# Two numbers per pass: fewer pairs of units block by block at the heads and tails of the input projections

## The chip, the cores and the metric

The kernel runs on one core of one Trainium2 chip. The metric is the device time of one execution in microseconds (us). The engines are named as the profile names them: PE is TensorE (PEld its weight loads), DVE is VectorE, ACT is ScalarE, POOL is GpSimd, SP is SyncE, which here only issues transfers.

## The reference

A trunk of two layers is applied with the same weights to two requests: a prompt of 512 tokens and a sample of 2048 tokens, each of width 1024.

```python
def trunk(x, ...):
    for l in range(DEPTH):                       # DEPTH = 2
        y = even_layer(x, w_in_even, ...) if l % 2 == 0 else odd_layer(x, w_in_odd, ...)
        x = layer_norm(ALPHA * x + y, ln_g[l], ln_b[l])

def even_layer(x, w_in, sink, w_out, t5_table):
    qa, ka, va, qb, kb, vb, ga, gb = _split(x @ w_in, EVEN_SPLITS)
    ...
    return concatenate([oa * silu(ga), ob * silu(gb)]) @ w_out

def odd_layer(x, w_in, rpb, lb, gnorm, w_out):
    qc, kc, vc, qd, idd, zf, zb, gc, gd = _split(x @ w_in, ODD_SPLITS)
    ...
    return concatenate([oc * silu(gc), od * silu(gd)]) @ w_out
```

What is left out is mixer A (windowed attention) and mixer B (dilated attention) in the even layer, mixer C (neighbourhood attention) and mixer D (HGRN2, both directions) in the odd one. This case concerns the first line of each layer, the combined input projection `x @ w_in`, in float32.

## The kernel before

**Tokens and units.** The 2560 tokens are 5 blocks of 512: block 0 is the prompt, blocks 1 to 4 are the sample. The columns of `w_in` are cut into units of 128, named after the reference's splits (`qb`, `kb`, ...; `v0`, `v1`, `v2` are value columns), and two units are a pair. Layer 0 has 14 pairs, layer 1 has 16.

**One pair.** A pair on a block is computed by seven matrix products of half size in place of eight (a fast scheme). x and the weights are each split into a high and a low float32r part, and each product takes three matmuls for each of four quarters of the contraction: 84 matmuls of 128 x 256 for a pair on one block, twice as many for a pair on two blocks (`pair_fm`, line 305; value pairs in `pair_v`, line 405). VectorE and ScalarE add the products out of PSUM (`products`, lines 270 to 281; the last additions are at lines 318 to 352): these are the evictions, and they cover one block (256 columns) or two (512).

**Weights.** `weights` (from line 160) is a generator that prepares the seven weight operands (`whl`) of a pair, in the order of the list `work`, into a pool of 6 tiles. The first time a pair comes, the raw weights are loaded, VectorE forms the sums, ScalarE and GpSimd split them (lines 106 and 107), and four of the seven prepared tiles, 512 KB each, are also written to DRAM. When the pair comes again, the four are read back (line 204), and of the raw weights 512 KB and 256 KB (lines 176 and 177); the other three operands are split anew. One preparation serves both blocks of a pair that runs on two.

**x.** `load_x` fills `xh` and `xl` of one block, seven forms of four quarters `k`, through a ring of two raw tiles. There are two such buffers, for even and odd blocks.

```python
        for k in range(4):
            r = raw(k)
            yield
            self.split(xh[:, k, :3], xl[:, k, :3], r[:, 1:])
            yield
            sums(k, r)
            yield
            self.split(xh[:, k, 3:], xl[:, k, 3:], r)
            yield
```

The raw load of 512 KB is issued at line 131 on SP; `split` is one instruction on ScalarE (line 106) and one on VectorE (line 107, tile `xl`, 128 x 768 and then 128 x 1024); `sums` are four subtractions on VectorE (lines 135 to 138). The generator advances two steps after each product (`tick`). The first two products of a pair (X11 and X21) need only the 128 x 768 parts.

**The order of the pairs.** `group` writes the part of the list for two blocks:

```python
        start[len(work)] = g[1]
        work += [(p, [b]) for b in g for p in pairs[:head]]
        work += [(p, list(g)) for p in pairs[head:len(pairs) - tail]]
        work += [(p, [g[0]]) for p in pairs[len(pairs) - tail:]]
        start[len(work)] = then
        work += [(p, [g[1]]) for p in pairs[len(pairs) - tail:]]
```

The first `head` pairs run on the first block alone, during which the second block's x is loaded, and then on the second block; the middle pairs run on both; the last `tail` pairs run on the first block, and then on the second, during which the next pass's first x (block `then`) is loaded into the buffer that came free. A pair in a head or tail is a *step* of 84 matmuls, and its weights are prepared twice. Each layer has a pass over blocks 0 and 1, one over 2 and 3, and then block 4 alone, whose steps a scheduler mixes with mixer A (layer 0) or mixer D (layer 1). The instructions' order on each engine is set by the scheduler from the program's order; transfers all stand in SP's queue in that order.

Of the kernel before, what the change touches and what calls it, by code (L numbers as in the profile page):

```python
# [67 lines left out]
def drain(g):  # L68
    for _ in g:
        pass  # L70


class Trunk:
# [1244 lines left out]
    def layer0(self):  # L1318
        pj, p0, p1, px, ma, bk, bw = (ExitStack() for _ in range(7))
        self.rp = self.pool(pj, "rp0", 2, side="left")  # L1320
        self.proj_pools(pj, 0, "left")
        x = [self.pool(e, f"x{i}", 1, side="left") for i, e in enumerate((p0, p1))]
        self.more_ps(p1, 0, "left")
        ring = self.pool(px, "xr0", 2, side="left")
        pair = {n: self.pairs(0, (n,)) for n in ("qa", "ka", "ga", "kb", "v0", "v2", "qb", "gb")}
        pairs = pair["v2"] + pair["kb"][2:3] + pair["kb"][0:1] + pair["kb"][1:2] + pair["ga"] + pair["gb"] + pair["v0"] + pair["qa"] + pair["ka"] + pair["qb"]
        work, start = [], {}
        self.group(work, start, (0, 1), pairs, 4, 3, 2)
        self.group(work, start, (2, 3), pairs, 4, 3, 4)
        work += [(p, [4]) for p in self.pairs(0, ("kb", "ga", "v0", "qa", "ka", "gb", "v2", "qb"))]  # L1330
        xs = {}
        load = lambda b: self.load_x(0, b, x[b % 2], [ring], xs)
        with ExitStack() as e:
            x0 = self.load_x(0, 0, x[0], [ring, self.pool(e, "xs", 2, side="right")], xs)
            self.proj_begin(0, work, {i: (lambda b=b: load(b)) for i, b in start.items()})
            next(x0)
            self.wq += [next(self.wgen), next(self.wgen)]
            drain(x0)
        self.side = self.side_work()
        n = len(work) - len(pairs)  # L1340
        self.proj(0, n, xs)
        while 4 not in xs:
            self.tick()
        px.close()
        p1.close()
        self.pss.pop()
        self.lbt = self.lower_bounds(self.const)
        self.gn = self.const.tile([P, 4], F32, name="gn")
        self.nc.sync.dma_start(self.gn, self.A["gn"])
        drain(self.side)  # L1350
        self.proj(0, len(pairs), xs)
        p0.close()
        pj.close()
        self.mixer_a(ma)
        ma.close()
        self.b_open(bk)
        self.b_work(bw)
        with ExitStack() as s:
            b = self.mixer_b(((1, 2), (1, 1), (0, 2), (0, 1), (0, 0), (1, 0)))
            for _ in range(24):  # L1360
                next(b)
            self.out_open(s, 0, "right", range(6))
            drain(b)
            bw.close()
            self.out_work(s, 0, "right")
            out = self.output(0)
            cb, ob = ExitStack(), ExitStack()
            self.ob = self.pool(ob, "o_b", 2, side="right")
            comb = self.b_combine(cb)
            next(comb)  # L1370
            for i in range(1, NB):
                next(comb)
                for _ in range(4):
                    next(out)
            drain(comb)
            cb.close()
            bk.close()
            self.p1 = ExitStack()
            self.x = [self.pool(self.p1, "y0", 1, side="left")]
            self.rp = self.pool(self.p1, "rp1", 2, side="left")  # L1380
            self.xr = self.pool(self.p1, "xr1", 2, side="left")
            self.plan1()
            x0 = self.load_x(1, 0, self.x[0], [self.xr], self.xs)
            for _ in range(4):
                next(out)
                for _ in range(4):
                    next(x0, None)
            drain(x0)
            ob.close()
            self.wp = self.pool(self.p1, "wp1", 6, side="left")  # L1390
            self.wq.insert(0, self.next_w())
            drain(out)

    def plan1(self):
        self.cd, self.cc = self.pairs(1, ("zb", "v1", "zf", "qd", "gd")), self.pairs(1, ("kc", "v0", "qc", "gc"))
        work, start, self.xs = [], {}, {}
        order = self.pairs(1, ("kc", "gc", "zb", "zf", "gd", "v0", "v1", "qc", "qd"))
        self.group(work, start, (0, 1), order, 3, 4, 2)
        self.group(work, start, (2, 3), order, 3, 4, 4)
        work += [(p, [4]) for p in self.cd + self.cc]  # L1400
        load = lambda b: self.load_x(1, b, self.x[b % 2], [self.xr], self.xs)
        self.proj_begin(1, work, {i: (lambda b=b: load(b)) for i, b in start.items()})
# [129 lines left out]
```

## Time and profile before

| | |
|---|---|
| median of 3 runs | 3397.63 us (3362.09 to 3405.03) |
| the profiled execution | 3397.89 us |
| its span | 3396.1 us |
| TensorE busy | 3158.8 us, 93% |
| VectorE busy | 2135.2 us, 63% |
| ScalarE busy | 1350.9 us, 40% |
| GpSimd busy | 1292.4 us, 38% |
| DMA | 765.35 MB, 225 GB/s in the mean |
| mean granted clock of TensorE | 0.958 |

The busy time of an engine is the sum of its instructions; matmuls are pipelined, so a busy TensorE is not always one at its best rate. What the table can't tell is where TensorE stands still; for that the stretches around the borders of the passes are looked at apart. The clock is given as a share of the full 2.4 GHz; the lower level is 1.2 GHz, 0.5.

### The profile page before, as it was taken

To read this page: it belongs to the slowest core of one execution; us is meant where nothing else is said; L and a number is where in the kernel's file an instruction comes from. 1 tells how busy PE (TensorE), PEld (TensorE's weight loads), DVE (VectorE), ACT (ScalarE), POOL (GpSimd) and SP (SyncE) were. 2 spreads that over 40 slices of the span, in tenths; PEclk is the share of its full clock that TensorE was granted. 3 is DMA by queue.
4 is the path that set the end of the run, shared out by engine and by line. 5 is a ranking of instruction groups with operands and counts; after the bars stand their busy time and mean duration, and the time that the engine had idled before them with its cause. 6 is when DMAs were issued, how large, how long until landed. Compare 5 with 4: busy or idle time off the path is not lost.

```text
span 3396.1 us, 71726 instructions
## 1 busy us (share of the span) xinstructions
PE 3158.8 (93%) x26922; PEld 2711.5 (80%) x26922; DVE 2135.2 (63%) x5201; ACT 1350.9 (40%) x3182; POOL 1292.4 (38%) x1041
## 2 busy tenths in 40 slices
PE   6999689979999999999799999999889888989998
PEld 5999689977776566677699999999879866666787
DVE  8555533257666454599965475332797788885576
ACT  4323321235455565412333233211333367777510
POOL 6446341322221010055554463212464544343244
PEclk9999899989999787999899999999999989999999
DMA  6857995799988377546575599557979885545443
GB/s 244 292 209 263 316 344 198 261 285 260 264 233 221 92 184 165 143 153 216 195 295 207 209 327 350 200 192 258 339 259 315 299 237 141 147 135 174 136 145 113
DMA packets 518048, 765.35 MB, mean 225 GB/s; under 512 B 72923, under 2 KB 331611, under 8 KB 517447
## 3 DMA queue, kind: packets, MB, share of 16 engines
q1 hardware_dynamic: 494023, 739.79, 68.2%
q10 hardware_dynamic: 23680, 20.97, 1.8%
q8 instruction: 215, 3.52, 0.4%
q14 instruction: 130, 1.06, 0.1%
HBM read 529.09 MB, written 231.54 MB: 224 GB/s over the span
## 4 chain that ended last, share of the span: by engine, by line
PE 44%; DVE 13%; DMA 5%; issue 3%; ACT 2%; POOL 1%; SPq 0%; DVEq 0%; POOLq 0%; ACTq 0%
PE acc L305 16%; PE oacc L969 7%; PE acc L405 6%; PE bpv L705 3%; PE bpt L689 2%; DMA whl<-wk_f 2%; PE bs L661 2%; DVE dQ L1248 2%; PE cs L1083 1%; PE bs L660 1%; PE cpv L1115 1%; DMA dF<-fm_zf 1%; DVE dT L1237 1%; PE bs L671 1%; PE cpt L1100 1%
## 5 line engine op out<-in xcount | busy, mean ns | idle before, releaser
L305 PE MATMUL acc<-xh,whl 128*128 128x256 f32 x7560 | 1431.5, 288 | 109.9 <-DMA whl<-wk_f 53.6
L305 PEld LDWEIGHTS acc<-xh,whl 128*128 128x128 f32 x7560 | 1211.1, 195 | 135.6 <-issue 75.6
L305 PE MATMUL acc<-xl,whl 128*128 128x256 f32 x3780 | 1081.4, 286 | 8.5 <-DVE xl L107 8.5
L107 POOL TENSOR_TENSOR whl<-wraw,whl 128x512 fp32r<-128x512 f32 x447 | 611.5, 1380 | 809.7 <-ACT whl L106 769.3
L305 PEld LDWEIGHTS acc<-xl,whl 128*128 128x128 f32 x3780 | 736.9, 195 | 10.2 <-DVE xl L107 10.1
L106 ACT ACTIVATE whl<-wraw 128x512 fp32r<-128x512 f32 x447 | 277.9, 628 | 435.3 <-PE acc L305 163.4
L969 PE MATMUL oacc<-wohl,yh 128*128 128x512 f32 x960 | 312.0, 406 | 5.6 <-ACT yh L106 3.4
L405 PE MATMUL acc<-whl,xh 128*128 128x256 f32 x1680 | 307.5, 285 | 2.9 <-POOL whl L107 2.8
L270 DVE TENSOR_TENSOR u<-acc,u 128x256 f32<-128x256 f32 (+1 forms) x279 | 147.0, 527 | 227.6 <-PE acc L305 142.7
L405 PEld LDWEIGHTS acc<-whl,xh 128*128 128x128 f32 x1680 | 262.8, 192 | 6.0 <-POOL whl L107 3.2
L1247 POOL TENSOR_TENSOR dK<-dK,dT 128x512 f32<-128x512 f32 x120 | 158.8, 1332 | 223.0 <-ACT dKm L1215 91.2
L405 PE MATMUL acc<-whl,xl 128*128 128x256 f32 x840 | 238.3, 284 | 0.0
L969 PEld LDWEIGHTS oacc<-wohl,yh 128*128 128x128 f32 x960 | 180.5, 190 | 52.3 <-ACT yh L106 4.7
L969 PE MATMUL oacc<-wohl,yl 128*128 128x512 f32 x480 | 189.2, 399 | 1.3 <-DVE yl L107 1.3
L983 POOL TENSOR_TENSOR res<-res,gb 128x1024 f32<-128x1024 f32 (+2 forms) x40 | 94.2, 2354 | 225.0 <-DVE res L976 145.2
L405 PEld LDWEIGHTS acc<-whl,xl 128*128 128x128 f32 x840 | 161.6, 192 | 0.1
L278 ACT ACTIVATE u<-acc 128x256 f32<-128x256 f32 (+1 forms) x124 | 55.9, 451 | 224.2 <-PE acc L305 192.8
L326 ACT ACTIVATE sg<-evc 128x512 f32<-128x512 f32 (+1 forms) x128 | 70.5, 551 | 184.2 <-DVE evc L318 158.3
L318 DVE TENSOR_TENSOR evc<-acc,u 128x512 f32<-128x512 f32 (+1 forms) x140 | 79.7, 571 | 89.0 <-PE acc L305 84.2
L681 ACT ACTIVATE bss<-bss,bstat 128x128 f32<-128x128 f32 (+2 forms) x240 | 107.2, 449 | 70.6 <-DVE bstat L679 70.3
L106 ACT ACTIVATE xh<-xraw 128x768 fp32r<-128x768 f32 (+1 forms) x80 | 73.7, 946 | 145.3 <-DVE xraw L138 89.2
L679 DVE CUSTOM_DVE_ANT_0 bss<-bs,btab 128x256 f32<-128x256 f32 (+2 forms) x224 | 72.0, 359 | 89.1 <-PE bs L661 53.8
(1026 smaller groups left out, 5646.6 us busy)
## 6 DMA issues: line engine op xcount, KB each, us to landing
whl<-wk_f SPq DMA_DIRECT2D x328, 512.0 KB
wk_f<-whl SPq DMA_DIRECT2D x108, 512.0 KB
wraw<-w SPq DMA_DIRECT2D x82, 512.0 KB
wraw<-w SPq DMA_DIRECT2D x26, 1024.0 KB
whl<-wk_v SPq DMA_DIRECT2D x48, 512.0 KB
wraw<-w SPq DMA_DIRECT2D x86, 256.0 KB
vtri<-vc_d SPq DMA_DIRECT2D x60, 240.0 KB
bq<-fm_qb SPq DMA_DIRECT2D x50, 256.0 KB
```

The source lines that it names most:

```text
L106: nc.scalar.activation(h, src, AF.Copy)
L107: (eng_l or nc.vector).tensor_sub(l, src, h.bitcast(F32))
L270: nc.vector.tensor_add(d, a, u)
L305: nc.tensor.matmul(accs[0][:, i * 256:(i + 1) * 256], w[:, wi, k * P:(k + 1) * P], xv[:, k, x], start=(k == 0 and j == 0), stop=(k == 3 an ...
L318: nc.vector.tensor_add(c, a, u)
L405: nc.tensor.matmul(acc[:, t * 256:(t + 1) * 256], xv[:, k, x, t * P:(t + 1) * P], w[k // 2][:, wi, k % 2 * 256:(k % 2 + 1) * 256], start=( ...
L679: nc.vector.tensor_tensor_reduce(ss[h][:, i, :nk], sc[h][:, i, so[i]:so[i] + nk], tb[:, hh, :], 1.0, BIG, ALU.add, ALU.min, mcol)
L681: nc.scalar.activation(ss[h][:, i, :nk], ss[h][:, i, :nk], AF.Exp, scale=-1.0, bias=mcol, accum_out=stt[:, t, hh, 1:2])
L705: nc.tensor.matmul(pvt[64 * h:64 * h + 64, t - t4], v[:cn, h * 64:h * 64 + 64], pts[h][:cn, i, ci], start=(ci == 0), stop=(ci == len(chunk ...
L969: nc.tensor.matmul(acc, yv, wo[c][:, wi, cs], start=(c == chunks[0][0] and i == 0), stop=(c == chunks[-1][0] and i == 2))
L983: e.tensor_mul(r[:, c0:c1], r[:, c0:c1], gb[:, 0, c0:c1])
L1247: nc.gpsimd.tensor_mul(km, km, of(T_, nb + 1, -(nb + 1), 2, 0))
```

## The change

Only the numbers `head` and `tail` are changed: in the first call of `group` the tail alone, in the other three both.

```diff
--- before.py
+++ after.py
@@ -1325,8 +1325,8 @@
         pair = {n: self.pairs(0, (n,)) for n in ("qa", "ka", "ga", "kb", "v0", "v2", "qb", "gb")}
         pairs = pair["v2"] + pair["kb"][2:3] + pair["kb"][0:1] + pair["kb"][1:2] + pair["ga"] + pair["gb"] + pair["v0"] + pair["qa"] + pair["ka"] + pair["qb"]
         work, start = [], {}
-        self.group(work, start, (0, 1), pairs, 4, 3, 2)
-        self.group(work, start, (2, 3), pairs, 4, 3, 4)
+        self.group(work, start, (0, 1), pairs, 4, 2, 2)
+        self.group(work, start, (2, 3), pairs, 2, 2, 4)
         work += [(p, [4]) for p in self.pairs(0, ("kb", "ga", "v0", "qa", "ka", "gb", "v2", "qb"))]
         xs = {}
         load = lambda b: self.load_x(0, b, x[b % 2], [ring], xs)
@@ -1395,8 +1395,8 @@
         self.cd, self.cc = self.pairs(1, ("zb", "v1", "zf", "qd", "gd")), self.pairs(1, ("kc", "v0", "qc", "gc"))
         work, start, self.xs = [], {}, {}
         order = self.pairs(1, ("kc", "gc", "zb", "zf", "gd", "v0", "v1", "qc", "qd"))
-        self.group(work, start, (0, 1), order, 3, 4, 2)
-        self.group(work, start, (2, 3), order, 3, 4, 4)
+        self.group(work, start, (0, 1), order, 2, 2, 2)
+        self.group(work, start, (2, 3), order, 2, 2, 4)
         work += [(p, [4]) for p in self.cd + self.cc]
         load = lambda b: self.load_x(1, b, self.x[b % 2], [self.xr], self.xs)
         self.proj_begin(1, work, {i: (lambda b=b: load(b)) for i, b in start.items()})
```

In layer 0 the pass over blocks 0 and 1 has one step pair fewer in its tail, and the pass over 2 and 3 two fewer in its head and one fewer in its tail. In layer 1 each pass has one fewer in its head and two fewer in its tail. So 4 pairs of layer 0 and 6 of layer 1 now run over both blocks, with one preparation of weights in place of two. The number of matmuls stays the same. All transfers of weights that are left out are counted on SP: 40 of line 204 (512 KB), 10 of line 176 (512 KB) and 10 of line 177 (256 KB).

SP, layer 0, from the pass over blocks 0, 1 to that over 2, 3. `whl<-wk_f_0_n_m` are the reads of prepared weights (m grows by one within a pair: 3477 is the last pair of the tail, 142 the first of the next head), `xraw<-xT` the raw loads of block 2's x, whose first two quarters were issued in the pair ahead. Before:

```order
L204 DMA whl<-wk_f_0_2_3309 128x1024
L204 DMA whl<-wk_f_0_3_3310 128x1024
L376 DMA fm_qb<-evh 128x512 x2
L376 DMA fm_qb<-evo 128x512 x2
L176 DMA wraw<-w 128x1024
L177 DMA wraw<-w 128x512
L204 DMA whl<-wk_f_0_0_3477 128x1024
L499 DMA etab<-rz_d 32x14x48 x4
L131 DMA xraw<-xT 128x2x512
L204 DMA whl<-wk_f_0_1_3478 128x1024
L131 DMA xraw<-xT 128x2x512
L204 DMA whl<-wk_f_0_2_3479 128x1024
```

After (3565 to 3568 is the last pair of the tail here):

```order
L204 DMA whl<-wk_f_0_2_3567 128x1024
L499 DMA etab<-rz_d 32x14x48
L204 DMA whl<-wk_f_0_3_3568 128x1024
L499 DMA etab<-rz_d 32x14x48
L374 DMA fm_qb<-evh 128x4x128 x2
L374 DMA fm_qb<-evo 128x4x128 x2
L176 DMA wraw<-w 128x1024
L177 DMA wraw<-w 128x512
L204 DMA whl<-wk_f_0_0_142 128x1024
L131 DMA xraw<-xT 128x2x512
L204 DMA whl<-wk_f_0_1_143 128x1024
L131 DMA xraw<-xT 128x2x512
```

Before, quarters 2 and 3 of x are issued among the weights of the last step of the tail; now they are issued among those of the first step of the next head, which is the step that reads that x.

VectorE, layer 1, in the load of block 3's x while the first pairs run on block 2. `xl` are the low parts of a quarter, lines 135 to 138 the sums, `u` and `evo` (lines 270 and 345) the evictions of a step, seven in all. Before:

```order
L345 TENSOR_TENSOR evo<-acc,u 128x256 x3
L270 TENSOR_TENSOR u<-acc,u 128x256 x3
L107 TENSOR_TENSOR xl<-xraw,xh 128x768
L135 TENSOR_TENSOR xraw<-xraw 128x256
L136 TENSOR_TENSOR xraw<-xraw 128x256
L137 TENSOR_TENSOR xraw<-xraw 128x256
L345 TENSOR_TENSOR evo<-acc,u 128x256
L138 TENSOR_TENSOR xraw<-xraw 128x256
L345 TENSOR_TENSOR evo<-acc,u 128x256 x2
L107 TENSOR_TENSOR xl<-xraw,xh 128x768
L107 TENSOR_TENSOR xl<-xraw,xh 128x1024
```

After:

```order
L270 TENSOR_TENSOR u<-acc,u 128x256
L345 TENSOR_TENSOR evo<-acc,u 128x256 x3
L107 TENSOR_TENSOR xl<-xraw,xh 128x768
L135 TENSOR_TENSOR xraw<-xraw 128x256
L136 TENSOR_TENSOR xraw<-xraw 128x256
L137 TENSOR_TENSOR xraw<-xraw 128x256
L138 TENSOR_TENSOR xraw<-xraw 128x256
L107 TENSOR_TENSOR xl<-xraw,xh 128x1024
L107 TENSOR_TENSOR xl<-xraw,xh 128x768
L135 TENSOR_TENSOR xraw<-xraw 128x256
L136 TENSOR_TENSOR xraw<-xraw 128x256
L345 TENSOR_TENSOR evo<-acc,u 128x256
```

Before, six evictions stand ahead of the third quarter and three more inside it, as the steps of the head go on; now four stand ahead of it, none inside it, and the sums of the fourth quarter begin with no eviction between.

## Rows read from the trace of the kernel before

**Rows 1.** The page, busy us, share of the span and instructions by engine.

```profile
PE 3158.8 (93%) x26922; PEld 2711.5 (80%) x26922; DVE 2135.2 (63%) x5201; ACT 1350.9 (40%) x3182; POOL 1292.4 (38%) x1041
```

**Rows 2.** Table of stretches: span, busy us (count) PE, PEld, DVE, ACT, POOL; clock, DMA, GB/s.

```profile
332.00:395.00 63.00, 36.78 (x259) 35.83 (x258) 29.79 (x49) 15.51 (x24) 14.97 (x12) 0.78 0.86 263
395.00:500.00 105.00, 92.58 (x734) 90.85 (x734) 54.52 (x89) 32.53 (x54) 52.38 (x39) 0.97 1.03 361
675.00:725.00 50.00, 43.03 (x332) 42.23 (x332) 34.46 (x58) 18.96 (x30) 16.41 (x12) 0.93 0.93 331
1675.00:1750.00 75.00, 67.13 (x519) 65.43 (x520) 54.51 (x86) 31.10 (x55) 43.88 (x30) 0.94 0.91 330
1968.00:2117.00 149.00, 140.95 (x1158) 139.19 (x1157) 91.27 (x175) 54.66 (x91) 77.80 (x56) 1.00 0.97 351
2381.00:2425.00 44.00, 41.52 (x344) 41.17 (x344) 30.86 (x61) 15.62 (x24) 16.89 (x12) 1.00 0.96 345
2150.00:2250.00 100.00, 100.00 (x835) 100.00 (x835) 37.42 (x55) 23.93 (x40) 18.71 (x15) 1.00 0.57 198
```

**Rows 3.** Waits of TensorE from 332 to 395: us in all, times, longest.

```profile
PE acc L305 <- DMA whl<-wk_f: 25.8, 3, 15.5
```

**Rows 4.** Tile xl, each load: ns min/median/max, first and last start, forms.

```profile
L107 DVE TENSOR_TENSOR xl<-xraw,xh x8: 951/1214/2047, 333.4 to 372.3; 128x768 fp32r<-128x768 f32 x4, 128x1024 fp32r<-128x1024 f32 x4
L107 DVE TENSOR_TENSOR xl<-xraw,xh x8: 943/1215/2412, 395.9 to 429.0; 128x768 fp32r<-128x768 f32 x4, 128x1024 fp32r<-128x1024 f32 x4
L107 DVE TENSOR_TENSOR xl<-xraw,xh x8: 950/1217/1639, 688.4 to 718.2; 128x768 fp32r<-128x768 f32 x4, 128x1024 fp32r<-128x1024 f32 x4
L107 DVE TENSOR_TENSOR xl<-xraw,xh x8: 1209/1453/2053, 1687.1 to 1717.2; 128x768 fp32r<-128x768 f32 x4, 128x1024 fp32r<-128x1024 f32 x4
L107 DVE TENSOR_TENSOR xl<-xraw,xh x8: 945/1120/1226, 2009.5 to 2038.4; 128x768 fp32r<-128x768 f32 x4, 128x1024 fp32r<-128x1024 f32 x4
L107 DVE TENSOR_TENSOR xl<-xraw,xh x8: 947/1082/1226, 2054.4 to 2083.1; 128x768 fp32r<-128x768 f32 x4, 128x1024 fp32r<-128x1024 f32 x4
L107 DVE TENSOR_TENSOR xl<-xraw,xh x8: 948/1084/1225, 2382.7 to 2410.5; 128x768 fp32r<-128x768 f32 x4, 128x1024 fp32r<-128x1024 f32 x4
```

**Rows 5.** The page, DMA issues: prepared weights read back, how many.

```profile
whl<-wk_f SPq DMA_DIRECT2D x328, 512.0 KB
```

**Rows 6.** The page, costliest groups: busy, mean ns of one, idle before.

```profile
L107 POOL TENSOR_TENSOR whl<-wraw,whl 128x512 fp32r<-128x512 f32 x447 | 611.5, 1380 | 809.7 <-ACT whl L106 769.3
L270 DVE TENSOR_TENSOR u<-acc,u 128x256 f32<-128x256 f32 (+1 forms) x279 | 147.0, 527 | 227.6 <-PE acc L305 142.7
```

**Rows 7.** Chain of waits at the head of layer 1: start, us, what.

```profile
1679.02 4.96 PE acc L305 x24
```

**Rows 8.** Table of stretches: behind the gap at B, and at the head of C.

```profile
710.00:720.00 10.00, 7.86 (x45) 7.86 (x46) 8.99 (x16) 4.12 (x7) 0.00 (x0) 0.66 0.72 247
1675.00:1685.00 10.00, 8.19 (x43) 7.82 (x44) 4.62 (x8) 2.63 (x5) 4.64 (x4) 0.57 0.95 290
```

**Rows 9.** Tile xraw: the first subtraction of the x sums (line 135), ns min/median/max.

```profile
L135 DVE TENSOR_TENSOR xraw<-xraw x38: 411/1138/1597, 7.9 to 2405.5; 128x256 f32<-128x256 f32 x38
```

**Rows 10.** Stretches, line 858 (score pairs of mixer A): beside block 4, after it.

```profile
750.00:1055.00 305.00, 46.91 (x113) 22.19 (x113) 0.97 0.89 247
1055.00:1140.00 85.00, 20.73 (x47) 9.34 (x47) 0.94 0.72 166
```

**Rows 11.** Stretches, line 305 (projection matmuls) beside mixer A.

```profile
750.00:1055.00 305.00, 131.55 (x974) 120.98 (x975) 0.97 0.89 247
```

**Rows 12.** Stretches, line 405 (projection matmuls of value pairs) beside mixer A.

```profile
750.00:1055.00 305.00, 21.67 (x168) 20.48 (x168) 0.97 0.89 247
```

**Rows 13.** Stretches, line 1221 (mixer D): beside block 4, after it.

```profile
2430.00:2730.00 300.00, 3.50 (x224) 2.68 (x224) 0.97 0.86 289
2730.00:3090.00 360.00, 7.68 (x416) 5.70 (x416) 0.95 0.57 160
```

## Prediction

> **What bounds the kernel now.** The page's busy shares come first: TensorE is busy 3158.8 us, 93% of the span [rows 1]. So the end is set by TensorE, and time can be won or lost only where TensorE stands still. I then cut the table of stretches around each place where a pass over two blocks ends and the next x must be loaded. In the quiet middle of a pass 835 matmuls end in 100 us, 0.1198 us each, at full clock and a DMA share of 0.57 [rows 2]; there TensorE is the only limit. At the five boundaries I take the stretch less its matmuls times 0.1198 as lost time:
> - A, layer 0 from blocks 0, 1 to 2, 3 (332 to 500): 168 − 993 × 0.1198 = 49.1 us
> - B, layer 0 to block 4: 50 − 332 × 0.1198 = 10.2
> - C, head of layer 1: 75 − 519 × 0.1198 = 12.8
> - D, layer 1 from 0, 1 to 2, 3: 149 − 1158 × 0.1198 = 10.3
> - E, layer 1 to block 4: 44 − 344 × 0.1198 = 2.8
>
> Together 85.2 us, with a DMA share of 0.86 to 1.03 in all of them [rows 2]. The waits of TensorE say what ends the loss at A: 25.8 us for prepared weights that are read back, one wait of 15.5 [rows 3]. The reader should see two different needs at a boundary: weights, which the block by block steps fetch twice, and x, whose load those same steps cover.
>
> How long a load of x takes is read from VectorE's eight low-part subtractions in it, from the first start to the last start plus 1.2 us: 40.1 and 34.3 at A, 31.0 at B, 31.3 at C, 30.1 and 29.9 at D, 29.0 at E [rows 4]. The mean of the seven is 31.5 when A's first is counted halfway (35.1) between 40.1 and 30.1, since the 15.5 us wait fell in it.
>
> **The change part by part.** *Work removed.* Ten pairs pass from block by block to two blocks (four in layer 0, three of them at A; six in layer 1). Each loses one second preparation: four 512 KB reads of prepared weights and raw reads of 512 and 256 KB, 2.88 MB. The order shows 40 of the 328 prepared reads gone [rows 5], 28.8 MB in all, and 30 splits each on GpSimd (30 × 1.38 = 41 us) and ScalarE [rows 6]. Matmuls stay the same in number. In the middle of a pass this preparation lies beside 0.57 of DMA and a full TensorE, so taking it away is worth 0 there; it counts only at boundaries.
>
> *Cover removed.* A pair on one block is 84 matmuls, 10.06 us. After the change each load that stood behind three or four such steps has two, 20.1 us. The first two products of the next pair (24 matmuls, 2.9 us) read only the first part of x, so a load of length L leaves TensorE idle for L − 23.0. Two loads back to back (tail 2, head 2) leave 2L − 43.1. With the lengths of before:
> - A: 40.1 + 34.3 − 43.1 = 31.3, or with 30.1 as the first 21.3; I take 26.3, so −22.8 against 49.1. The lower end that bytes allow: 63 us at 263 and 105 at 361 GB/s are 54.5 MB [rows 2]; less 3 × 2.88 this is 45.9, at 361 GB/s 127 us, where the matmuls need 119: 8 lost at least
> - B: 31.0 − 23.0 = 8.0, so −2.2
> - C: the head starts at 1679.0 [rows 7], 8.1 before the load's first subtraction, and 1675 to 1685 loses 10 − 43 × 0.1198 = 4.9 in any case [rows 8]. 31.3 + 8.1 + 4.9 − 23.0 = 21.3, so +8.5
> - D: 60.0 − 43.1 = 16.9, so +6.6
> - E: 29.0 − 23.0 = 6.0, so +3.2
>
> Sum −6.7.
>
> *The clock behind a stall.* After the gap at B, 710 to 720 shows a granted clock of 0.66, near the lower of the two levels, and 45 matmuls in 7.86 busy us, where full rate makes 65.6: 2.5 us [rows 8]. Six stalls (A two, the others one each) give +15.0. The ends are 0, if the stalls come in pieces, and 15.
>
> *Fewer evictions inside a load.* VectorE makes seven evictions of 0.527 us per step [rows 6], 3.7 us, in the same queue as the load's subtractions. One step fewer runs inside each load. VectorE is busy in 34.46 of 50 us at B [rows 2], so part of this is idle anyway: between 0 and 3.7 a load, I take half, 7 × 1.85 = −13.0.
>
> The load's own subtraction, two reads from SBUF, shows 411 ns at least and 1597 at most [rows 9]. The Trainium skill, "SBUF — State Buffer", section "SBUF: two separate sides", says that VectorE and GpSimd hold their shared port as an exclusive lock for an instruction. By it a subtraction waits for one GpSimd split at most, 411 + 1380 = 1791, and the trace's 1597 agrees; three splits fewer in each of seven loads would be worth up to 7 × 4.1 = 29 us, and the sum would be 3372 as an estimate by that page.
>
> *Mixers that share TensorE with block 4.* The order decides how much of a mixer is still to do when the last projection ends. For mixer A it is now 63 of 160 score pairs in place of 47. Those 47 took 85 us alone, 1.81 each; interleaved, 113 took 305 − (974 + 168) × 0.1198 = 168.2, 1.49 each [rows 10 to 12]. 16 × 0.32 = +5.1. For mixer D one chunk tile of 20 more is left. Before, 7 tiles (32 records of line 1221 each) pass beside the projections and 13 after them in 360 us, 27.7 each [rows 13]; if a moved tile loses the same part of its pace as in mixer A, 0.32 of 1.49, that is 6, and nothing if mixer C's work fills the place; I take +3.0. Sum +8.1.
>
> *The sum.* −6.7 + 15.0 − 13.0 + 8.1 = +3.4. The profiled execution took 3397.9 us (span 3396.1), and the median of the three runs is 3397.6 (3362.1 to 3405.0), so the base needs no shift: **3401 us**. As a formula with L' for the mean load after the change: 7 L' − 204.3, with L' = 31.5 − 1.85 = 29.7. Every us of load is worth 7, and the sign turns at 29.2.
>
> **The rivals.** *Loads shorten, and A falls to its bytes.* VectorE's own work in an undisturbed load is 4 × (0.95 + 4 × 0.41 + 1.2) = 15.2 us [rows 4, 9]; halfway to 31.5 is about 24. Then B loses 1.0, C 14.0, D 4.9, E 1.0 and A its 8: 28.9 against 85.2 is −56.3. With the mixers' +8.1 and one slow clock at C (+2.5) that is −45.7: 3352 us. For it speak the removed reads at shares near 1; against it that D and E, with no long wait for weights, show 29 to 30 us all the same.
>
> *Other side: x comes too late with two steps of cover.* If the load's raw reads, in SP's one queue behind the reads of the next pair's weights, stay as late as at A's first load, L' is 40.1: 7 × 40.1 − 204.3 = +76, 3474 us. It decides from L' = 29.2 on, and is over 2% (68 us, about what a measurement of this kernel can tell from no change) from 38.9. For it speaks that the raw reads of the last two quarters keep their places between the same weights in SP's order, one step nearer to their use; against it that six of seven loads are shorter.
>
> *Nothing shows.* Weights and x may simply trade one wait for the other at a full DMA, so that the boundaries keep their 85 us: 3398. The Trainium skill, "Perfetto Trace Analysis", section "Identifying Performance Opportunities", says that improving a kernel generally involves its most-contended engine. By that rule this change, which leaves TensorE its instructions, gives 3398; the trace agrees that TensorE is the one, at 93%, but the 85 us are that engine's idle time.
>
> **How the numbers follow.** The boundary sum as above 0.52, with a range of its own of 3380 to 3422 (L' three us either way, 7 each); loads that shorten 0.17; x too late 0.16; nothing shows 0.15. The range takes in the likeliest and the middle case whole, the first rival's price as its low end, 3352, and goes half way to the second's, 3450. Faster by over 2% (under 3330) is not even reached by the gain's own price; 0.03 for it. Slower by over 2% (over 3466) needs most of the second rival: 0.07. Within 2%: 0.90.
>
> **What would show it.** Right: the 15.5 us wait for weights at A is gone and 332 to 500's work takes some 20 us less; at B to E TensorE stands 6 to 21 us in front of the first product of the next pass, waiting for x, with a lower clock behind it; loads of about 30 us; the matmuls as many as before; 288 prepared reads. Wrong: loads at D and E under 26 or over 35 us; a long wait for weights that stays at A; the time from the last projection of block 4 to mixer A's end not some 29 us longer (16 pairs at 1.81); or a boundary at which VectorE holds evictions back behind x that has not landed, so that TensorE stops before its cover is used up.

## The result: 0.9% slower, inside the range, with a base and a change that were both off

The changed kernel takes 3406.2 us in the median of 20 executions, the kernel before 3375.7 in the median of 20: a ratio of 1.009, with a 95% interval of 1.0061 to 1.0119. A second set of 12 executions gave 1.0091 (1.0054 to 1.0127). The forecast of 3401 us within 3352 to 3450 and of "within 2%" came true. But it was +3.4 us on a base of 3397.9, and the measured change is +30 on a base of 3375.7. The profiled execution of before was 22 us above the median; why is shown below. One execution of the changed kernel took 7177.4 us; the ratios use each kernel's executions within about 1.5% of its fastest, and of the profiles below those of e3, e4 and e8 lie above that, so their stretches count only where others show the same.

The profiled execution of the changed kernel took 3396.6 us with a span of 3394.8. Its page, as [rows 1] and [rows 5]:

```profile
PE 3142.1 (93%) x26922; PEld 2707.4 (80%) x26922; DVE 2111.7 (62%) x5143; ACT 1329.6 (39%) x3122; POOL 1259.3 (37%) x1019
...
whl<-wk_f SPq DMA_DIRECT2D x288, 512.0 KB
```

TensorE keeps its 26,922 instructions, and 40 reads of prepared weights are gone, as the change says. The five boundaries in the table of stretches, columns as in [rows 2], each with about as many matmuls as there:

```profile
332.00:495.00 163.00, 130.41 (x995) 127.77 (x994) 80.12 (x126) 44.78 (x68) 72.64 (x54) 0.91 0.91 295
670.00:717.00 47.00, 40.22 (x330) 39.50 (x328) 28.51 (x47) 18.77 (x29) 21.10 (x14) 0.99 0.97 339
1644.00:1722.00 78.00, 68.78 (x512) 65.42 (x512) 50.30 (x75) 29.36 (x46) 39.42 (x27) 0.93 0.76 278
1941.00:2094.00 153.00, 143.92 (x1157) 140.97 (x1157) 84.26 (x161) 48.21 (x76) 62.59 (x47) 0.99 0.80 289
2358.00:2400.00 42.00, 41.50 (x346) 41.33 (x345) 23.37 (x48) 13.37 (x22) 15.83 (x12) 1.00 0.95 329
```

Less 0.1198 us per matmul, the losses are 43.8 at A (49.1 before), 7.5 at B (10.2), 16.7 at C (12.8), 14.4 at D (10.3) and 0.5 at E (2.8). TensorE's longest waits in A (us in all, times, longest), first before, from 332 to 500, then changed, from 332 to 495:

```profile
PE acc L305 <- DMA whl<-wk_f: 34.4, 7, 15.5
```

```profile
PE acc L305 <- DMA whl<-wk_f: 12.9, 5, 7.4
PE acc L305 <- DVE evo L343: 11.2, 3, 7.7
```

The longest wait for weights fell from 15.5 us to 7.4, but 11.2 us of waits for evictions came. The longest of these, 7.7 us up to 349.5, had a wait for transfers behind it, which e4 explains. VectorE waited for ScalarE's copy `evh` of an output, and ScalarE for outputs in SP's queue (from 332 to 352 and to 350):

```profile
DVE evo L107 <- ACT evh L106: 10.0, 2, 9.0
```

```profile
ACT evh L106 <- DMA fm_qb<-evo: 7.1, 1, 7.1
```

The loads of x, as [rows 4]:

```profile
L107 DVE TENSOR_TENSOR xl<-xraw,xh x8: 945/1090/2424, 355.8 to 385.9; 128x768 fp32r<-128x768 f32 x4, 128x1024 fp32r<-128x1024 f32 x4
L107 DVE TENSOR_TENSOR xl<-xraw,xh x8: 944/1224/1544, 396.7 to 426.8; 128x768 fp32r<-128x768 f32 x4, 128x1024 fp32r<-128x1024 f32 x4
L107 DVE TENSOR_TENSOR xl<-xraw,xh x8: 952/1217/1482, 694.9 to 722.5; 128x768 fp32r<-128x768 f32 x4, 128x1024 fp32r<-128x1024 f32 x4
L107 DVE TENSOR_TENSOR xl<-xraw,xh x8: 957/1220/1983, 1656.8 to 1683.2; 128x768 fp32r<-128x768 f32 x4, 128x1024 fp32r<-128x1024 f32 x4
L107 DVE TENSOR_TENSOR xl<-xraw,xh x8: 949/1082/1226, 2002.5 to 2030.5; 128x768 fp32r<-128x768 f32 x4, 128x1024 fp32r<-128x1024 f32 x4
L107 DVE TENSOR_TENSOR xl<-xraw,xh x8: 948/1225/2308, 2036.5 to 2060.6; 128x768 fp32r<-128x768 f32 x4, 128x1024 fp32r<-128x1024 f32 x4
L107 DVE TENSOR_TENSOR xl<-xraw,xh x8: 952/1082/1224, 2379.7 to 2407.6; 128x768 fp32r<-128x768 f32 x4, 128x1024 fp32r<-128x1024 f32 x4
```

With 1.2 us behind the last start they last 31.3 (the first; its own last subtraction took 2.4, so 32.5), 31.3, 28.8, 27.6, 29.2, 25.3 and 29.1 us: 29.1 in the mean, where the forecast had L' = 29.7.

**Where the time went.** One execution each says little here, since the granted clock differs between executions of one kernel. So both kernels were profiled twice, and the span was cut at the same work: projection matmuls (lines 305 and 405) were counted in stretches of 5 us (those that lie across two stretches are scaled out, so that they sum to 13,860), and mixers were cut at their first and last matmuls. Cuts at each matmul's own start give the same within about 1.5 us. Times in us:

| stretch | before | again | changed | again | difference of means |
|---|---|---|---|---|---|
| A, matmul 2016 to 3360 | 215.6 | 217.9 | 209.3 | 209.5 | −7.4 |
| B, 4536 to 5040 | 71.4 | 73.4 | 71.6 | 73.2 | 0.0 |
| block 4 of layer 0 and mixer A | 419.5 | 412.8 | 422.3 | 418.4 | +4.2 |
| mixer B | 279.9 | 243.2 | 245.2 | 246.0 | by the clock |
| rest of layer 0, to layer 1's first matmul | 231.6 | 233.0 | 237.3 | 237.0 | +4.9 |
| C, from there to 7300 | 147.4 | 149.4 | 151.0 | 151.3 | +2.8 |
| D, 8400 to 9924 | 193.7 | 191.6 | 197.7 | 197.1 | +4.7 |
| E, 11500 to 12348 | 104.6 | 104.5 | 102.5 | 102.4 | −2.1 |
| block 4 of layer 1, with mixer D | 302.8 | 301.8 | 308.8 | 308.0 | +6.1 |
| mixers C and D behind it | 500.7 | 509.0 | 516.1 | 514.8 | +10.6 |
| layer 1's output | 168.0 | 168.0 | 170.7 | 170.7 | +2.7 |
| all the rest | 760.9 | 766.3 | 762.4 | 765.1 | +0.2 |

Without mixer B the sum is +26.7 us. Most stretches repeat within 3 us; mixer B does not. The same instructions of it in the kernel before, in its two profiled executions, and in the run e3 (columns as in [rows 2], the clock third from the right):

```profile
1146.00:1426.00 280.00, 279.95 (x1604) 185.17 (x1602) 133.48 (x666) 155.14 (x560) 17.64 (x13) 0.82 0.65 150
```

```profile
1149.00:1392.00 243.00, 241.97 (x1602) 162.24 (x1601) 132.93 (x665) 154.51 (x564) 17.63 (x13) 0.98 0.79 174
```

```profile
1148.00:1488.00 340.00, 339.72 (x1602) 221.36 (x1602) 134.14 (x664) 155.38 (x562) 17.60 (x13) 0.64 0.53 124
```

The count of matmuls is the same and TensorE is busy throughout; only the clock differs, 0.82, 0.98 and 0.64, and the time goes from 243 to 340 us. This stretch alone put the first profile of before 37 us above the second, and its 97 us are about as wide as the spread of all times of before (3355 to 3449). It is left out where variants are compared below.

### The profile page after: what moved, and what is told of

It reads as the page before. It is cut to its first block, busy times and chain, and to the rows that moved or that the text cites. A ratio compares the mean times of both kernels' runs of the same rounds, so it can differ in the third digit from the quotient of the medians.

```text
span 3394.8 us, 71250 instructions
## 1 busy us (share of the span) xinstructions
PE 3142.1 (93%) x26922; PEld 2707.4 (80%) x26922; DVE 2111.7 (62%) x5143; ACT 1329.6 (39%) x3122; POOL 1259.3 (37%) x1019
## 4 chain that ended last, share of the span: by engine, by line
PE 35%; DVE 10%; DMA 4%; issue 2%; ACT 2%; POOL 1%; SPq 0%; DVEq 0%; ACTq 0%; POOLq 0%
PE acc L305 17%; PE oacc L969 7%; PE acc L405 6%; DVE dQ L1248 2%; PE cs L1083 1%; PE cpv L1115 1%; DVE dT L1237 1%; PE cpt L1100 1%; DVE css L1090 1%; DVE xl L107 1%; DVE datt L1260 1%; DMA whl<-wk_f 1%; DMA dF<-fm_zf 1%; DVE rs_t L1009 1%; DVE rs_y L1010 0%
## 5 line engine op out<-in xcount | busy, mean ns | idle before, releaser
L305 PE MATMUL acc<-xh,whl 128*128 128x256 f32 x7560 | 1445.4, 290 | 112.4 <-DMA whl<-wk_f 28.8
L107 POOL TENSOR_TENSOR whl<-wraw,whl 128x512 fp32r<-128x512 f32 x417 | 562.4, 1357 | 843.2 <-ACT whl L106 786.4
L106 ACT ACTIVATE whl<-wraw 128x512 fp32r<-128x512 f32 x417 | 259.5, 628 | 443.1 <-PE acc L305 179.3
L969 PEld LDWEIGHTS oacc<-wohl,yh 128*128 128x128 f32 x960 | 181.6, 190 | 46.0 <-issue 2.4
L107 POOL TENSOR_TENSOR whl<-wsum,whl 128x512 fp32r<-128x512 f32 x66 | 94.3, 1431 | 81.5 <-ACT whl L106 62.6
```

Of the source, the lines that this page charges most:

```text
L106: nc.scalar.activation(h, src, AF.Copy)
L107: (eng_l or nc.vector).tensor_sub(l, src, h.bitcast(F32))
L305: nc.tensor.matmul(accs[0][:, i * 256:(i + 1) * 256], w[:, wi, k * P:(k + 1) * P], xv[:, k, x], start=(k == 0 and j == 0), stop=(k == 3 an ...
L969: nc.tensor.matmul(acc, yv, wo[c][:, wi, cs], start=(c == chunks[0][0] and i == 0), stop=(c == chunks[-1][0] and i == 2))
```

## The experiments

Every experiment was timed against the kernel before on the same chip; e7 and e8 have up to 6 more lines, so their line numbers differ.

### e5 and e6: both kernels once more

No edit. 

> The kernel before once more, for a second profile of the same order of instructions. The first profile and the ones of the variants differ by up to 95 us in mixer B (245 to 340 us) at granted clocks from 0.97 to 0.64, with the same instructions; if that is the chip's clock and not the kernel, mixer B takes another time here than 279.9. The stretch of mixers C and D behind block 4's projections took 498 us before and 512 to 529 in all five variants, two of which leave layer 1 alone: if the scheduler's order of before is a better one, it takes 498 to 505 again; if it is the clock too, it may come out at 510 or more. The boundaries A to E repeat within 2 us if they belong to the kernel.

> The changed kernel once more, for a second profile. Between the same matmuls as before: A 209 (6 less than before), D 198 (4 more), block 4 with mixer D 311 (5 more), each within 2 us; behind them mixers C and D 510 to 518 where an order of its own is the cause, or 498 to 505 in a quick state of the clock if it is that alone. Ratio to before 1.006 to 1.012.

Measured: ratios of 0.9981 (0.9945 to 1.0017) and 1.0091 (1.0054 to 1.0127), and the second columns of the table above. For before, A to E came out within 3 us, and so belong to the kernel. The start up to matmul 2016 (298.6 and 303.9), block 4 with mixer A, mixer B, and mixers C and D (500.7 and 509.0, at granted clocks of 0.97 and 0.95) did not. The 509.0 lies between the two cases that were expected, so this run alone leaves it open whether order or clock sets mixers C and D.

### e1 and e2: one layer each

```diff
-        self.group(work, start, (0, 1), pairs, 4, 3, 2)
-        self.group(work, start, (2, 3), pairs, 4, 3, 4)
+        self.group(work, start, (0, 1), pairs, 4, 2, 2)
+        self.group(work, start, (2, 3), pairs, 2, 2, 4)
```

> Only layer 0 has the new heads and tails; layer 1 is as before. By the prediction's sum this half alone should gain: A -22.8, B -2.2, clock +7.5, evictions -7, mixer A +5, together some -20 us (ratio 0.994). The rival, read from the two traces: A lost 54.6 us before and 48.2 after between the same matmuls, because the tables' small transfers stand in the way there and not the weights, and mixer A gives 3 us back; then this half is worth -2 to -6 us, ratio 0.998 to 1.000, and A still loses over 40 us in its profile.

Measured 1.0100 (1.0042 to 1.0159), so neither theory: no gain of 20 us, and no zero. A took 211.0 us (before 216.8 in the mean), as in the changed kernel. But mixers C and D, in a layer that the edit does not touch, took 528.2 in place of 504.9, and the rest of layer 0 237.5 in place of 232.3.

```diff
-        self.group(work, start, (0, 1), order, 3, 4, 2)
-        self.group(work, start, (2, 3), order, 3, 4, 4)
+        self.group(work, start, (0, 1), order, 2, 2, 2)
+        self.group(work, start, (2, 3), order, 2, 2, 4)
```

> Only layer 1 has the new heads and tails. By the prediction's sum +8.5 (C), +6.6 (D), +3.2 (E), +7.5 clock, -7 evictions, +3 mixer D: some +20 us, ratio 1.006. The rival, read from the two traces: C +9, D +4, E and what follows it +20 or more, because mixer D does less beside block 4's projections and catches up behind them: +30 to +36 us, ratio 1.009 to 1.011, so all of what the whole change costs.

Measured 1.0162 (1.0101 to 1.0222), nearer to the rival. D took 197.4, block 4 with mixer D 309.1 (both as in the changed kernel), and mixers C and D 533.6. The two halves cost 1.0% and 1.6% and the whole 0.9%: they don't add up, so something other than the boundaries is in each of them.

### e3, e10 and e9: tails of 2, heads of 2, and heads of 4 in layer 1

```diff
-        self.group(work, start, (0, 1), order, 3, 4, 2)
-        self.group(work, start, (2, 3), order, 3, 4, 4)
+        self.group(work, start, (0, 1), order, 3, 2, 2)
+        self.group(work, start, (2, 3), order, 3, 2, 4)
```

> Layer 1 with heads of 3 as before and tails of 2 as in the change, layer 0 as before. If the loss of layer 1 sits at the tails (E and what mixer D does beside block 4), this keeps nearly all of it, +20 us or more, and C costs nothing. If it sits at the heads (C's late x, 8.1 us behind the first matmul), this costs at most 10 us, ratio under 1.003.

Measured 1.0119 (1.0054 to 1.0185). C stayed at 147.1, D took 196.7, block 4 with mixer D 313.8, mixers C and D 518.8: the tails, with the new order behind them, carry layer 1's loss.

e10 has `2, 4` in both lines, the heads alone. 

> Layer 1 with the changed heads (2) and the tails of before (4), layer 0 as before. With the run that changed the tails alone this splits layer 1. Heads alone: C loses 3 us more than before (about 9 in place of 6) since its x is late by one step; E with block 4 stays as before (304 to 106), where tails alone cost 11; D between 9 and 12 lost, since six steps still cover two loads of 60 us less 2.9. Ratio 1.000 to 1.006 if mixers C and D come out 10 us worse as in the other variants.

Measured 0.9997 (0.9946 to 1.0048). C lost 9.3 us between matmuls 6468 and 7300 (before 6.3 and 5.2), as expected of one step less cover, D 11.3, and block 4 took 301.2. Mixers C and D took 500.8, as before. In this variant alone of those so far the scheduler left their order of instructions exactly as it was.

e9 has `4, 4` in both lines, so its heads are one longer than before and its tails the same. 

> The other way: layer 1 with heads and tails of 4 in both passes (heads were 3, tails 4), layer 0 as before. If cover for x is what the head of layer 1 lacks (31.3 + 8.1 - 23.0 with two steps, 6.3 with three, none with four), the loss between matmuls 6468 and 7300 falls from 5 or 6 us to 0 to 1. D (8400 to 9924) has cover enough already with seven steps; if more steps only read more prepared weights there, its loss stays at 9 to 11 us or grows by 2 to 4. Loads of x keep 29 to 31 us. In all within 5 us of before but for mixers C and D, whose order comes out anew: ratio 0.999 to 1.006.

Measured 1.0104 (1.0061 to 1.0147). C lost 14.9 us, not 0 to 1: with one step more, the head of layer 1 loses more, not less. TensorE's waits there name evictions (8.1 us, before 2.9) and prepared weights (3.4, before 1.3), and none names x. That the second preparation of weights costs more than the cover is worth fits this but is not shown; the model by which a step of cover returns what x lacks failed at C. D lost 13.3, as expected. Mixers C and D: 523.0.

### e4 and e7: the tables that stand in the way at A

What stops TensorE at A can be read in the trace of before. The DMA's busy tenths and its GB/s, in 40 slices of 330 to 350:

```profile
DMA  7596444544458985444544699745994894799979
GB/s 261 130 302 140 51 46 51 56 51 46 51 56 199 275 199 56 51 46 51 56 51 46 124 183 210 224 130 209 262 291 115 172 221 188 274 373 328 279 254 369
```

The queues are four to five tenths busy for much of that time and move about 50 GB/s. SP's issues at the start of it (start, duration, line, what):

```profile
328.18 1.07 SPq L491 DMA_DIRECT2D rz_d<-rp  x1
329.30 1.17 SPq L374 DMA_DIRECT2D fm_qb<-evo  x1
330.56 5.06 SPq L215 DMA_DIRECT2D wk_f<-whl  x1
335.71 4.87 SPq L176 DMA_DIRECT2D wraw<-w  x1
```

At 328.2 a table for mixer C is written to DRAM, `rz_d`, from 8 partitions (line 491, a piece of side work that runs one step per pair). Its 256 packets of 2560 bytes, 655 KB in all, start between 330.2 and 343.3, which is 50 GB/s. Two of the three issues behind it take 5 us each, where lines 215 and 176 took 0.3 to 1.1 just ahead, and the weights for which TensorE waits 15.5 us [rows 3] stand in the same queue. The changed kernel has the same write at 327.2.

```diff
     def side_work(self):
-        for _ in range(9):
+        for _ in range(3):
             yield
```

> The kernel before, with the side work (bias tables, one step per pair) begun 3 pairs from the start in place of 9, so that the tables' small transfers fall in the middle of the first pass and not at its end. If they are what stops TensorE at A from 330 to 350, the loss between matmuls 2268 and 2520 falls from 32 us to 12 or less, and the time by 15 to 25 us (ratio 0.993 to 0.996). If prepared weights are the limit there (as the prediction took it), the loss stays at 28 us or more and the ratio at 1.000.

Measured 0.9971 (0.9922 to 1.0019), so not told apart from before. A fell from 216.8 to 186.7 us, so the tables are the cause; but the stretch up to matmul 2016 grew by 17 to 22, as it seems because the tables now meet the first preparation of weights there.

```diff
             for r0, r1 in ((0, 8), (8, 15)):
+                nc.gpsimd.tensor_copy(rp[:1, :1], self.last[:1, 0, 0, :1])
                 nc.gpsimd.memset(rp, 0.0)
...
         yield from self.bias_vectors()
-        yield from self.rpb_tables()
+        for _ in range(11):
+            yield
+        t = self.rpb_tables()
+        while next(t, t) is not t:
+            next(t, None)
+            yield
```

> The kernel before, with layer 0's bias tables (small transfers to and from DRAM) held back by a copy that needs a later pair's result, so that they run in the middle of the pass over blocks 2 and 3, where the DMA share is 0.57. If they are what stops TensorE at A, A (between matmuls 2016 and 3360) takes 186 to 192 us in place of 215.6, as where they came earlier, the stretch to matmul 2016 stays at 299 (it took 321 there), and the middle of the pass (141.1) grows by less than 10: 15 to 25 us in all, ratio 0.993 to 0.996. If prepared weights and x are the limit at A, A stays over 205.

Measured 0.9964 (0.9912 to 1.0015), so not told apart from before either. A took 184.8 (−32), the middle of the pass 149.7 (+8.6). TensorE in the same 993 or so matmuls that stand in [rows 2], and its waits there:

```profile
336.00:471.00 135.00, 123.55 (x994) 122.02 (x993) 79.50 (x139) 48.49 (x79) 47.79 (x34) 0.97 0.99 353
```

```profile
PE acc L305 <- DVE evo L343: 5.7, 2, 3.9
PE acc L305 <- DMA whl<-wk_f: 3.6, 3, 2.0
```

135 less 994 × 0.1198 is 15.9 us lost in place of 49.1, with heads and tails as they were, and the longest wait for weights is 2.0. The slow queue went along with the table, which is written at 485.4 here (`wv` are raw weights of a value pair):

```profile
485.42 0.30 SPq L492 DMA_DIRECT2D rz_d<-rp  x1
486.90 0.32 SPq L376 DMA_DIRECT2D fm_ga<-evo  x1
490.12 2.25 SPq L176 DMA_DIRECT2D wraw<-wv  x1
492.42 4.99 SPq L177 DMA_DIRECT2D wraw<-wv  x1
```

That is shown: most of A's loss was the tables, not the weights that are read twice. Of the gain of 24 the end kept little, as mixers C and D took 524.2.

### e8: the changed layer 0 without the tables in its way

The edit of e7 with a wait of 6, and layer 0 as in e1. 

> Tables held back as in the run beside it, and layer 0 with the changed heads and tails (4, 2 and 2, 2); layer 1 as before. If the gain that the prediction saw at A is real but hidden by the tables, A falls below that of the run beside it by up to the 8 to 10 us that two loads with four steps of cover leave; if four steps are too few cover without the tables, A comes out higher by 5 to 20 us (2 x 30 - 43.1 = 17 lost at least). Together a ratio of 0.990 to 0.998, unless the order of mixers C and D behind it comes out 10 to 20 us worse, as in the other variants.

Measured 0.9996 (0.9953 to 1.0039). A took 180.4, against 184.8 in e7, and the middle 152.5 against 149.7: neither a gain of 8 to 10 nor a loss of 5 to 20. Once the tables are away, the change of layer 0 is worth about 2 us there, no more than such stretches differ between executions of one kernel. Mixers C and D: 525.3.

### e11 and e12: the order of mixers C and D

The scheduler decides the order by a simulated time line, so an edit anywhere ahead may change how mixers C and D interleave. Of TensorE's order behind block 4's last projection, with D for the 16 small matmuls of one tile of mixer D (line 1221) and c12 for 12 score matmuls of mixer C (line 1083), the kernels' listings read:

```
before, e10   D c12 D c6 D c10 D c7 D c10 D c8 D c10 D c8 D c11 D c8 D c10 D c6 D c54
e1            D c11 D c8 D c10 D c7 D c11 D c7 D c11 D c7 D c11 D c7 D c10 D c6 D c54
changed  D c4 D c11 D c8 D c11 D c7 D c10 D c7 D c10 D c8 D c10 D c7 D c10 D c6 D c51
```

The differences look small. To test whether they are what costs, heads and tails of layer 1 were picked for which TensorE's order of both mixers comes out exactly as in before. e11 is e7 (with a wait of 10) and this; e12 is e8 with `2, 3` and `2, 4`.

```diff
-        self.group(work, start, (0, 1), order, 3, 4, 2)
-        self.group(work, start, (2, 3), order, 3, 4, 4)
+        self.group(work, start, (0, 1), order, 2, 2, 2)
+        self.group(work, start, (2, 3), order, 2, 4, 4)
```

> The tables held back to the middle of layer 0's second pass, layer 0's heads and tails as before; in layer 1 heads of 2, tails of 2 in the first pass and 4 in the last. These numbers were picked because mixers C and D come out in exactly the order of before. If that order is what cost the other variants 10 to 25 us behind block 4's projections, this stretch takes 498 to 508 us here, where the same tables with another order took 520.7; if it is the tables or the clock, it takes 512 or more. With A at 185 (before 216.8), the middle of the pass 8 longer, C +3 and D +4: ratio 0.990 to 0.996.

> Tables held back, layer 0 with the changed heads and tails, in layer 1 heads of 2 and tails of 3 and 4; again mixers C and D in exactly the order of before. The stretch behind block 4's projections takes 498 to 508 us if the order decides, 512 or more if not (524.1 with the same layer 0 and another order). A 180 to 182, the middle +11, C +3, D +2: ratio 0.989 to 0.996, the shortest of all if both hold.

Measured: e11 0.9935 (0.9890 to 0.9979), as expected, e12 1.0026 (0.9988 to 1.0063), not as expected. The stretch of mixers C and D, from the last projection matmul to the last matmul of line 1115, in all 14 profiles:

| order of C and D as in before | us | another order | us |
|---|---|---|---|
| before | 500.7 | changed | 516.1 |
| e5 before again | 509.0 | e6 changed again | 514.8 |
| e10 heads of layer 1 | 500.8 | e1 layer 0 | 528.2 |
| e11 tables, 2/2, 2/4 | 499.9 | e2 layer 1 | 533.6 |
| e12 tables, layer 0, 2/3, 2/4 | 509.9 | e3 tails of layer 1 | 518.8 |
| | | e4 tables early | 513.4 |
| | | e7 tables late | 524.2 |
| | | e8 tables late, layer 0 | 525.3 |
| | | e9 fours | 523.0 |

The rows from which this is taken, of matmuls of the projections (line 305, from 2600 on) and of mixer C (line 1115, which is 1121 in e7): x count, ns min/median/max, first and last start. The first two are of e7, the other two of e11.

```profile
L305 PE MATMUL acc<-xh,whl x208: 277/283/583, 2602.0 to 2671.5; 128*128 128x256 f32 x104
```

```profile
L1121 PE MATMUL cpv<-cpts,vtri x1920: 220/222/370, 2699.3 to 3195.7; 120*64 120x64 f32 x166, 80*64 80x64 f32 x26
```

```profile
L305 PE MATMUL acc<-xh,whl x208: 278/283/552, 2600.4 to 2670.8; 128*128 128x256 f32 x104
```

```profile
L1115 PE MATMUL cpv<-cpts,vtri x1920: 216/222/369, 2695.7 to 3170.7; 120*64 120x64 f32 x166, 80*64 80x64 f32 x26
```

Both leave the projections at 2671; the one with before's order ends at 3170.7, the other at 3195.7. All five profiles with that order lie at 499.9 to 509.9, all nine with another at 513.4 to 533.6. But e12's 509.9 lies between the bounds that were expected (508 and 512), so the clock is still a rival. What separates the two is the time that TensorE stood still in the stretch, its span less PE's busy time (columns as in [rows 2]). Here is e5 with before's order, then e4 and e7 with another:

```profile
2694.20:3203.10 508.90, 459.96 (x6782) 336.13 (x6781) 382.33 (x1192) 347.13 (x943) 189.86 (x126) 0.95 0.56 159
```

```profile
2764.30:3277.60 513.30, 456.90 (x6782) 334.48 (x6781) 387.25 (x1195) 348.06 (x940) 187.56 (x126) 0.96 0.56 158
```

```profile
2671.80:3195.90 524.10, 462.24 (x6782) 337.32 (x6781) 388.85 (x1196) 348.50 (x939) 187.93 (x126) 0.95 0.55 155
```

TensorE has the same matmuls in all three, and e4 had the highest clock. Yet TensorE stood still for 48.9 us in e5, and for 56.4 and 61.9 in e4 and e7. Over all 14 profiles it is 45.8 to 49.4 us in the five and 53.4 to 64.5 in the nine. Within the five, where the matmuls are the same, the times go with the clock, 499.9 us at 0.97 to 509.9 at 0.95. Seven of the nine have 32 to 173 more matmul records in the stretch, as more of mixer D is left, so e4 and e7 are the clean ones. That the order decides is shown as far as 14 profiles can show it; which exchange in it costs what was not tried.

e11 is faster than both kernels, by 0.65% against before. A took 181.6 us in it. e12 has A at 179.1, but it is not told apart from before. Without mixer B its profile took 3118 us, 24 more than e11's 3094: mixers C and D 10 at the lower clock, the rest of layer 0 another 9 (233.8 and 225.1), block 4 with mixer D 4.

## Why the prediction was right, and where it was not

The number held by luck: two errors cancel. The base was taken from an execution 22 us above the median of before, and the text said that it needed no shift; the three times shown (3362, 3398, 3405) were 43 us apart and should have told that something swings. And the change was +27 to +30, not +3.4. The forecast named signs of being wrong, and several came: a wait for weights of 7.4 us stayed at A, a load at D took 25.3 us, and at B VectorE held an eviction back behind the load of x. They are told below with their terms.

- **Boundary A (−22.8, with clock and evictions −21.5): the step that failed.** Measured −7.4. It took the loss of 49.1 us for weights and x, since the waits name prepared weights [rows 3]. The weights were late for another reason, the tables' write in the same queue, and the change leaves that where it is (e4, e7). The wait names what came last, not what held it up.
- **"TensorE stands 6 to 21 us, waiting for x" at B to E: not so.** The longest waits at B, changed (670 to 735) and before (675 to 735), and the longest that name x in the changed kernel at D (1941 to 2094) and at E (2358 to 2430) are:

```profile
PE acc L305 <- DVE evo L343: 5.8, 1, 5.8
```

```profile
PE acc L305 <- DVE evo L343: 6.4, 1, 6.4
```

```profile
PE acc L305 <- ACT xh L106: 2.1, 4, 1.0
```

```profile
PE acc L305 <- ACT xh L106: 1.5, 1, 1.5
```

  With the waits for `xl` (0.6 and 0.8) that makes 2.7 us at D and 2.3 at E, in pieces of at most 1.5. At B TensorE stops 24 matmuls ahead of the pass's end, because the eviction stands behind the load of x on VectorE. Three rows of its time line (start, us, what, idle time before it):

```profile
711.73 1.48 DVE L107 TENSOR_TENSOR xl<-xraw,xh 128x768 fp32r<-128x768 f32 x1 [1.94 <-ACT xh L106]
...
717.25 1.22 DVE L107 TENSOR_TENSOR xl<-xraw,xh 128x1024 fp32r<-128x1024 f32 x1
718.38 0.57 DVE L343 SCALAR_TENSOR_TENSOR evo<-acc,u 128x256 f32<-128x256 f32 x1
```

  The kernel before has the same wait, 108 matmuls ahead.
- **B (−1.6 with clock and evictions).** Measured 0.0 by the same matmuls, −2.7 in the stretch: right in size, but by the wait just told and not by a wait for x.
- **C (+9.2 so).** Measured +2.8: its sign is right, its size too large. The load there took 27.6 us and not 29.5 (31.3 less 1.85). The head was also misread: it does not start at 1679.0. Its first 24 matmuls ran before, between layer 0's last transposes, from 1657.7 to 1665.1; this is the first of them:

```profile
1657.66 0.39 PE L305 MATMUL acc<-xh,whl 128*128 128x256 f32 x1
```

  So less cover was left behind 1679.0 than the sum had, which would make it 2.9 us larger and further off. In e1, where layer 1 is as before, C took 152.9, so its +2.8 may not be the cover's at all. And e9 shows that the cover model does not hold there in the other direction.
- **D (+5.4).** Measured +4.7: right in size. But the two loads took 54.5 us and not the 56.3 that the sum allows (60.0 less 3.7), and by the sum they leave 11.4 us, 13.9 with one slow clock, where 14.4 were lost.
- **E (+3.9).** −2.1 in the pass and +6.1 in block 4 behind it: right together. Of the 6.1 only 2.3 are waits that name x; the rest comes with the tails (e3 and e2 have it, e10 does not), and its cause is open.
- **The clock behind a stall (+15.0): not found at that size.** In the changed kernel, behind the passes' ends of B and E and in D's second load:

```profile
717.00:727.00 10.00, 7.99 (x52) 8.00 (x53) 7.16 (x15) 2.26 (x5) 0.89 (x2) 0.71 0.73 246
2040.00:2094.00 54.00, 48.10 (x368) 45.95 (x367) 28.51 (x48) 14.39 (x22) 15.01 (x11) 0.97 0.80 279
2400.00:2430.00 30.00, 22.07 (x140) 20.54 (x139) 22.54 (x45) 13.97 (x26) 10.00 (x11) 0.83 0.99 347
```

  A lower clock follows the stall at B (0.71), but it did so before too, 0.66 [rows 8]. At E (0.83) it follows the waits for x and one of 4.1 us for mixer D. At D (0.97) the waits came in pieces and it hardly fell. By these rows the clock cost 7.99 − 52 × 0.1198 = 1.8 us at B; no run shows the term by itself.
- **Loads: L' 29.7.** Measured 29.1. The size of the half that was taken for the evictions held, but no run tells the evictions' share from the one of GpSimd. VectorE's first subtraction of a sum (line 135) had a median of 1138 ns before [rows 9] and has 426 in the changed kernel:

```profile
L135 DVE TENSOR_TENSOR xraw<-xraw x38: 410/426/2026, 8.3 to 2401.7; 128x256 f32<-128x256 f32 x38
```

  The median says too much, since the times lie in two groups: with no GpSimd instruction beside it a subtraction of line 135 took at most 427 ns, and of 40 in all 25 took over 600 before and 18 in the changed kernel, every one beside a GpSimd instruction. (The longest of all, 2026 ns, lies in layer 0's output, beside a GpSimd instruction of 4.8 us.) So loads are less held up by GpSimd too, as the first rival had it; but they did not fall to 24.
- **Mixer A (+5.1).** Measured +4.2 with block 4's stretch, where the two profiles of before are 7 apart, so it is not contradicted. As forecast, 63 of the 160 score pairs stand behind the last projection in place of 47, but from there to mixer B it takes 22 us longer and not 29 (108.7 and 109.4, before 89.7 and 83.7).
- **Mixer D (+3.0): mis-sized.** Measured +10.6, of mixers C and D together. It was priced as one tile moved, and one did move. What also changed was the order of everything behind it, and e7 shows that at +19 with no tile moved at all.
- **Not seen:** the rest of layer 0 +4.9 (in e1 too, 237.5, so it comes with layer 0's new order) and layer 1's output +2.7 (in neither half alone). Their cause is open.

Of the rivals, "x too late" did not come (no load near 40 us), "loads shorten" came by 2.4 us in the mean and not by 7.5, and "nothing shows" was wrong by the 0.9%.

## What to carry to other kernels

A wait that names a transfer asks for one more look: what stood ahead of it in its queue, and how many GB/s moved meanwhile. Where a scheduler sets the order, an edit's price holds the new order of everything behind it, which the trace of before cannot show; compare the orders stage by stage, and judge an edit by a variant that has its neighbours' order kept. And before a sum of a few us is laid on one execution, profile the kernel twice and cut both at the same work: a stage that swings by 37 us is seen at once.

## What the runs showed of the hardware

Mixer B ran the same 1602 to 1604 matmul records in 243, 280 and 340 us at granted clocks of 0.98, 0.82 and 0.64, with TensorE busy for all but 1 us of it each time. The first two are the same kernel; what decides the clock there is open. And one write of a table from 8 partitions held the DMA at about 50 GB/s, with its engines half busy, and two of SP's next three issues at 5 us each, while TensorE stood still for 15.5 us; where the table was moved (e7), the slow issues went along (4.99 us). A subtraction of line 135 on VectorE (128 x 256) took 0.41 to 0.43 us with no GpSimd instruction beside it in the first profiles of the two kernels, and 1.3 and 1.4 us in the median with one.
